# Tokens turned before their norm, three passes per half of a projection, and a list scheduler that is run again with latest times

## The chip, the cores and the metric

The kernel runs on one core of a Trainium2 chip. The metric is device time in microseconds of one execution; the time of a kernel is the median of several runs. The profile is of one further execution. Its engines are TensorE (PE; PEld is its weight load), VectorE (DVE), ScalarE (ACT), GpSimd (POOL) and SyncE (SP), which issues most transfers.

## The reference

One layer of a hybrid encoder is computed for two groups of tokens at once: 512 prompt tokens and 64 sample tokens, of width 1024, with shared weights.

```python
xn = _rmsnorm(x, p['ln_mix'])                 # x * rsqrt(mean(x*x) + EPS) * gain
proj = xn @ p['w_in']
conv_in, z, a, b, qd, kd, vd = jnp.split(proj, SPLIT_AT, axis=-1)
c, conv_new = _causal_conv(conv_in, p['conv_w'], conv_buf)
...
oa, S_new = _gdn_chunked(qa, ka, va, g, beta, S0)
...
ob = _diff_attention(qd, k_all, v_all, q_pos, k_pos, lam)
...
h = x + jnp.concatenate([oa, ob], axis=-1) @ p['w_out']
h = h + _mem_attn(_rmsnorm(h, p['ln_mem_q']), mem_k, mem_v, p['w_mem_q'], p['w_mem_o'])
hn = _rmsnorm(h, p['ln_ffn'])
h = h + jnp.square(jax.nn.relu(hn @ p['w_ff1'])) @ p['w_ff2']
```

The input projection has 3592 columns: twelve blocks of 128 for the convolution, four for the gate z, eight single columns for a and b, and twelve blocks for queries, keys and values of the attention. The norm of x is a factor per token, times a gain per feature.

## The kernel before

**Precision and layout.** Everything is in 32 bits. For a projection, weights w and inputs x are each split into a high and a low part (a cast to `fp32r` on ScalarE, a subtraction on VectorE), and high by high, high by low and low by high are summed in a PSUM bank. Inputs lie features by tokens: a 128-column weight block is the stationary operand, and the 576 tokens are streamed. `KT = 8` blocks k of 128 features are summed (`kt=4` in the second feed-forward product, which goes by groups of 512 features).

**A projection** (`project`, L463) goes by two halves of the tokens, `HALVES`: 0 to 255, and 256 to 575 (the last 64 are the sample). In the first half, `high_parts` (L479) streams the high and low inputs side by side, 2 by 256 columns, through one load of the high weight into a whole bank, and a second matmul of 256 columns adds low weight by high input. The eviction receives two sums, `b` and `more`, and adds them: `add_to` (L487) copies one on ScalarE and adds the other on VectorE. In the second half three matmuls of 320 columns go into one sum. The first feed-forward product (`ff1_pair`, L1767) is a scheme of its own with 288 columns per matmul; it is not edited.

**The opening** (L540 to L724) is written out by hand, `with in_order()`: each engine keeps the written order. Tokens are loaded five tiles at a time row by row (`load_x`), and the gain is spread over partitions by a matmul. Per tile: squares (ScalarE, L517), root (L522, and a power on GpSimd, L502), scaling with factor and gain (VectorE, L527), four turns on TensorE per half of the features (`turn`, L529, through `tr`, L411), and the split into high (`hi`, L582) and low (`lo`, L587). `first` multiplies three convolution blocks (4, 5 and 6) with the first 256 tokens as soon as these are there; `second` does their other 320 tokens. The convolution input leaves PSUM by copies on ScalarE (L612, L616, L617).

**The raw tokens** are needed once more, turned, as the residual. `raw_out` (L575) copies turned raw tokens out of PSUM (L577). Two groups of turns stand in the opening (L665, L685), eight more in the block behind the key convolutions (L765 to L768). The result goes to a scratch tensor `hd` and is read back as `hT` (L1505) before the output projection.

**After the input projection** come the chunked recurrence (`gdn_prep`, `gdn_scan`), with the gate z projected in between, and the attention, one head at a time: `diff_project` (L1261) projects q, k and v, and splits keys into two copies whose halves are moved across partitions by transfers (L1309, L1311). Then memory keys and values, the output projection and the memory attention (`add_residual`, `split_query`), and the feed-forward part: `ff1_pair` and `project` by groups (`add_group`, L1834), the last group by `last_block` (L1871). The end turns the result back, scales it and stores it.

**What sets the order.** The program is traced in one order. `arrange` (L304) builds an `Arrangement` of all instructions with a cost for each (`Step.cost`, L102), and runs a list scheduler once: at each step it takes the engine that can start first, and among what can start there the instruction of the smallest priority, then of the smallest number. The priority is that of the trace; `tc.high_priority()` stands around casts of weights (L454) and most evictions. Tiles come from pools with a fixed number of buffers per tag; projections have three banks (`pr`), the others two or one. The order found is laid down by dependences.

## Time and profile before

| what | value |
|---|---|
| median of 3 runs | 958.92 us (957.37 to 960.45) |
| the profiled execution | 958.01 us, span 956.1 us |
| mean granted TensorE clock | 0.997 |
| matmuls | 6399 |
| TensorE, VectorE, ScalarE busy | 945.9, 690.8, 536.4 us |
| bytes moved by transfers | 96.01 MB |

The span runs from the first to the last instruction of the program; the execution's time is longer by what lies around it. A row of the timeline gives start, time, engine, line, operation, output and inputs with shapes, how many were merged, and, in brackets, how long the engine stood idle before and what ended that. A matmul's time in such a row is that of one pass through the array, and consecutive ones overlap; what one costs in a stream is the distance from start to start. `pr`, `ba`, `g` and `gs` are PSUM banks.

### The profile page before, as it was taken

To read this page: it belongs to the slowest core of one execution; us is meant where nothing else is said; L and a number is where in the kernel's file an instruction comes from. 1 tells how busy PE (TensorE), PEld (TensorE's weight loads), DVE (VectorE), ACT (ScalarE), POOL (GpSimd) and SP (SyncE) were. 2 spreads that over 40 slices of the span, in tenths; PEclk is the share of its full clock that TensorE was granted. 3 is DMA by queue.
4 is the path that set the end of the run, shared out by engine and by line. 5 is a ranking of instruction groups with operands and counts; after the bars stand their busy time and mean duration, and the time that the engine had idled before them with its cause. 6 is when DMAs were issued, how large, how long until landed. Compare 5 with 4: busy or idle time off the path is not lost.

```text
span 956.1 us, 17017 instructions
## 1 busy us (share of the span) xinstructions
PE 945.9 (99%) x6399; PEld 889.0 (93%) x6399; DVE 690.8 (72%) x1538; ACT 536.4 (56%) x1246; POOL 68.2 (7%) x158
## 2 busy tenths in 40 slices
PE   9999999999999999999999999999999999999996
PEld 7999899999899888999999999999999999999996
DVE  5666786878678776656557978668867779978574
ACT  6665675444567765444445568666555544555444
POOL 4351020202010000000000000000000000000000
PEclk9999999999999999999999999999999999999998
DMA  6562322122656656331212423333323322222202
GB/s 193 135 212 67 81 66 67 45 68 69 155 136 167 221 170 198 86 113 45 66 45 61 129 88 89 101 88 90 88 68 89 89 87 88 89 90 89 66 23 99
DMA packets 124915, 96.01 MB, mean 100 GB/s; under 512 B 6204, under 2 KB 112846, under 8 KB 124322
## 3 DMA queue, kind: packets, MB, share of 16 engines
q1 hardware_dynamic: 124466, 94.28, 34.0%
q8 instruction: 50, 0.82, 0.4%
q10 hardware_dynamic: 368, 0.66, 0.2%
q14 instruction: 31, 0.25, 0.1%
HBM read 79.93 MB, written 9.75 MB: 94 GB/s over the span
## 4 chain that ended last, share of the span: by engine, by line
PE 92%; DMA 2%; issue 2%; DVE 2%; ACT 1%; POOL 0%; SPq 0%; POOLq 0%; ACTq 0%; DVEq 0%
PE pr L407 57%; PE ba L407 12%; PE g L407 12%; PE gs L407 7%; PE ba L411 2%; PE g L411 2%; DMA KQ<-vb 1%; DMA Dt<-At 1%; DMA u<-in_x_prompt_dram 0%; DMA out_dram<-p 0%; PE pr L411 0%; DVE wl L456 0%; DVE p L755 0%; ACT u L1897 0%; PE gs L411 0%
## 5 line engine op out<-in xcount | busy, mean ns | idle before, releaser
L407 PE MATMUL pr<-u,wh 128*128 128x320 f32 (+2 forms) x1240 | 326.3, 341 | 0.0
L407 PE MATMUL pr<-u,wl 128*128 128x256 f32 (+1 forms) x816 | 225.5, 301 | 0.0
L407 PEld LDWEIGHTS pr<-u,wh 128*128 128x128 f32 x1240 | 211.2, 188 | 14.4 <-ACT u L582 0.4
L407 PEld LDWEIGHTS pr<-u,wl 128*128 128x128 f32 x816 | 149.9, 189 | 2.6 <-DVE wl L683 0.2
L456 DVE TENSOR_TENSOR wl<-raw,wh 128x1024 fp32r<-128x1024 f32 x65 | 79.5, 1223 | 50.2 <-ACT wh L455 49.8
L455 ACT CAST wh<-raw 128x1024 fp32r<-128x1024 f32 x65 | 68.2, 1049 | 74.4 <-PE pr L407 63.9
L407 PE MATMUL pr<-u,w2h 128*128 128x320 f32 (+1 forms) x384 | 96.7, 339 | 0.0
L1755 ACT CAST w2h<-r 128x512 fp32r<-128x512 f32 x56 | 34.6, 620 | 71.4 <-PE pr L407 69.2
L407 PE MATMUL pr<-f,w2h 128*128 128x320 f32 (+1 forms) x288 | 72.3, 339 | 0.0
L407 PEld LDWEIGHTS pr<-u,w2h 128*128 128x128 f32 x384 | 65.1, 188 | 4.3
L407 PE MATMUL pr<-u,w2l 128*128 128x256 f32 (+1 forms) x256 | 65.2, 295 | 0.0
L407 PE MATMUL ba<-u,wl 128*128 128x288 f32 x360 | 52.7, 295 | 0.0
L407 PEld LDWEIGHTS pr<-f,w2h 128*128 128x128 f32 x288 | 48.8, 188 | 3.3
L502 POOL TENSOR_TENSOR tiny<-tiny,nhalf 128x1 f32<-128x1 f32 (+4 forms) x10 | 8.5, 849 | 605.5 <-DVE tiny L1911 506.8
L1845 DVE TENSOR_TENSOR u<-u,pr 128x256 f32<-128x256 f32 x96 | 42.8, 446 | 11.2 <-PE pr L407 10.8
L407 PEld LDWEIGHTS ba<-u,wl 128*128 128x128 f32 x360 | 49.4, 188 | 0.0
L407 PE MATMUL pr<-f,w2l 128*128 128x256 f32 (+1 forms) x192 | 48.8, 295 | 0.0
L407 PEld LDWEIGHTS pr<-u,w2l 128*128 128x128 f32 x256 | 47.0, 189 | 1.5
L1756 DVE TENSOR_TENSOR w2l<-r,w2h 128x512 fp32r<-128x512 f32 x56 | 38.4, 686 | 10.2 <-ACT w2h L1755 10.1
L407 PE MATMUL pr<-wh,u 128*128 128x512 f32 x128 | 42.0, 399 | 0.0
L1515 DVE TENSOR_TENSOR u<-u,pr 128x256 f32<-128x256 f32 (+1 forms) x48 | 21.6, 451 | 20.4 <-PE pr L407 20.4
L407 PEld LDWEIGHTS pr<-f,w2l 128*128 128x128 f32 x192 | 35.2, 189 | 1.1
(551 smaller groups left out, 2024.7 us busy)
## 6 DMA issues: line engine op xcount, KB each, us to landing
raw<-in_w_ff_dram SPq DMA_DIRECT2D x36, 512.0 KB
raw<-in_w_in_dram SPq DMA_DIRECT2D x28, 512.0 KB
r<-in_w_ff_dram SPq DMA_DIRECT2D x56, 256.0 KB
raw<-in_w_mem_k_dram SPq DMA_DIRECT2D x8, 512.0 KB
raw<-in_w_mem_v_dram SPq DMA_DIRECT2D x8, 512.0 KB
raw<-in_w_out_dram SPq DMA_DIRECT2D x8, 512.0 KB
raw<-in_w_mem_q_dram SPq DMA_DIRECT2D x8, 512.0 KB
raw<-in_w_mem_o_dram SPq DMA_DIRECT2D x8, 512.0 KB
```

The lines of the kernel that those rows point to most:

```text
L407: nc.tensor.matmul(out, lhsT, rhs, start=start, stop=stop, skip_group_check=skip_group_check)
L411: nc.tensor.transpose(out, in_, ident[:n, :n])
L455: A.copy(wh, raw)
L456: V.tensor_tensor(wl, raw, wh.bitcast(F32), ALU.subtract)
L502: G.tensor_tensor(out, in_, bc(nhalf[: in_.shape[0], 0:1], list(in_.shape)), ALU.pow)
L1515: V.tensor_tensor(hm, hm, b, ALU.add)
L1755: A.copy(wh, src)
L1756: V.tensor_tensor(wl, src, wh.bitcast(F32), ALU.subtract)
L1845: V.tensor_tensor(am, am, b, ALU.add)
```

## The change

The tokens are turned raw, once. High and low parts are made from the turned raw tokens times the gain; the norm's factor per token is computed beside it (`roots_of`), spread over the partitions by a matmul into a row `rB`, and multiplied at each eviction of the input projection (`scaled`). The same turned banks give the residual's copy (`raw_rows`). The projection's inputs are stored in another order of tokens: 0 to 255, the 64 sample tokens, 256 to 511 (`XCOL`), so that the input projection's halves are 320 and 256 columns (`GATHERED`); all other projections have two halves of 288 (`EVEN`). Each half takes three matmuls per k into one sum, and evictions handle one sum. Tokens and the first weights are loaded in halves by features. The opening isn't fixed by hand any more. The decay rows and the sample's state take other slots.

The scheduler gets other costs (transfers by their row length, half speed of TensorE in the first 9 us), prefers a more urgent instruction that is about to be ready over one that is ready, and is run nine times: after each run the latest time of every instruction that isn't TensorE's becomes its priority, and the run with the earliest end is taken.

```diff
+EVEN = ((0, T // 2), (T // 2, T // 2))
+XCOL = (0, 128, 320, 448, 256)
+GATHERED = ((0, 320), (320, 256))
...
+COLD = 9000.0
...
+    def choose(self, engines):
+        start, engine = min((self.start(s), e) for e in engines for s in self.queue[e])
+        urgency = lambda s: (s.priority, s.n)
+        s = min((s for s in self.queue[engine] if self.start(s) <= start), key=urgency)
+        if engine in ("ACT", "DVE", "POOL") and not s.is_dma and not s.boundary and s.time >= 200:
+            end, soon = start + s.time - OVERLAP[engine], []
+            for t in self.queue[engine]:
+                wait = self.start(t) - start
+                if 0 < wait <= 600 and end - self.start(t) > 0.5 * wait and urgency(t) < urgency(s):
+                    soon.append(t)
+            s = min(soon, key=urgency, default=s)
+        return s
...
+        for s in reversed(order):
+            delay[s.n] = max((delay[n] + time for n, time in behind.get(s.n, ()) if place[n] > place[s.n]), default=0.0)
+        return {n: self.last[0] - d for n, d in delay.items()}
+
+    def improve(self, rounds):
+        best = self.run(), self.order
+        for _ in range(rounds):
+            for n, at in self.latest().items():
+                if self.steps[n].engine != "PE":
+                    self.steps[n].priority = at
+            best = min(best, (self.run(), self.order), key=lambda b: b[0])
+        return best[1]
...
-    for instructions_of_engine in Arrangement(instructions, homes, closing, opening, chains).run().values():
+    for steps in Arrangement(instructions, homes, closing, opening, chains).improve(8).values():
...
-    def project(w, x, evac, kt=KT, halves=HALVES, between=None):
+    def project(w, x, evac, kt=KT, halves=EVEN):
...
+                xk = x[k // 4][:, :, k % 4, a0 : a0 + n]
+                mm(b[:, :n], w[1][:, k, :], xk[:, 0], start=k == 0, stop=False)
+                mm(b[:, :n], w[0][:, k, :], xk[:, 0], start=False, stop=False)
+                mm(b[:, :n], w[0][:, k, :], xk[:, 1], start=False, stop=k == kt - 1)
+            evac(b[:, :n], a0, n)
...
+    load_rows_of(0, 0)
+    load_first(4, 0, 4)
+    load_rows_of(0, 1)
+    load_first(4, 4, 8)
+    nc.sync.dma_start(xu[2][:DEC, 0, :], x_sample[0])
+    load_first(5, 0, 8)
+    load_first(6, 0, 8)
+    for q in range(2):
+        load_rows_of(1, q)
...
+    def scaled(dst, b, at):
+        V.tensor_tensor(dst, b, rB[: dst.shape[0], at : at + b.shape[-1]], ALU.mult)
...
+        for i in range(nk):
+            A.activation(his[i], b[:, i], AF.Identity, scale=gmix[:, k0 + i : k0 + i + 1])
+        for i in range(nk):
+            V.scalar_tensor_tensor(los[i], b[:, i], gmix[:, k0 + i : k0 + i + 1], his[i].bitcast(F32), ALU.mult, ALU.subtract)
+
+    def raw_rows(b, ts, k0, nk, n):
+        t0 = TT[ts[0]][0]
+        for q in range(k0 // 4, (k0 + nk - 1) // 4 + 1):
+            ks = slice(max(k0, 4 * q), min(k0 + nk, 4 * q + 4))
+            dst = hst[q][:, ks.start - 4 * q : ks.stop - 4 * q, t0 : t0 + n]
+            (V.tensor_copy if len(held) % 2 else A.copy)(dst, b[:, ks.start - k0 : ks.stop - k0])
+
+    def roots_of(ts):
+        for t in ts:
+            n = TT[t][1]
+            r1 = root(squares(junk[t % 2], xt[t], n), n)
+            b = bank("gs")
+            mm(b[:, :n], bc(r1[:n], [n, P]), ident[:n, :n])
+            V.tensor_copy(rB[:, XCOL[t] : XCOL[t] + n], b[:, :n])
+
+    keep_busy(3)
...
+    keep_busy(4)
...
+    for q, tags in enumerate((("ba", "ba"), ("g0", "g1"))):
+        banks = [turn_rows((0, 1), 4 * q + 2 * i, 2, tag) for i, tag in enumerate(tags)]
+        early += banks
+        for x in banks:
+            split_rows(*x)
+        cast_first(4, q)
+        first(4, (HH, Q[q]), (LH, Q[q]), (HL, Q[q]))
+    roots_of((0, 1))
+    early.append(turn_rows((4,), 0, KT, "gs"))
+    split_rows(*early[-1])
+    for q in range(2):
+        cast_first(5, q)
+    for x in early:
+        raw_rows(*x)
+    roots_of((4,))
+    ev[4](fb[4][:, :256], 0, 256)
+    first(5, (HH, K), (HL, K), (LH, K))
+    ev[5](fb[5][:, :320], 0, 320)
+    for q in range(2):
+        cast_first(6, q)
+    for k0, tag in enumerate(("ba", "ba", "g0", "g1")):
+        x = turn_rows((2, 3), 2 * k0, 2, tag)
+        split_rows(*x)
+        raw_rows(*x)
+    first(6, (HH, K), (HL, K), (LH, K))
+    ev[6](fb[6][:, :320], 0, 320)
+    roots_of((2, 3))
+    second(4)
...
-            with after(opened[mybir.EngineType.PE], opened[mybir.EngineType.Activation]):
-                for q in range(2):
-                    for t in range(0 if q else 2, 5):
-                        raw_out(t, q, turn(xt[t], TT[t][1], q, f"g{t % 2}"))
...
-        def evac(b, a0, n, more):
+        def evac(b, a0, n):
             am = (accu[0] if g < SCALED else hT)[m // 4][:, m % 4, a0 : a0 + n]
...
+                if g == 0:
+                    A.copy(am, b)
+                else:
+                    V.tensor_tensor(am, am, b, ALU.add)
```

`turn_rows` turns one or two token tiles for a range of features into one bank; `cast_first` splits half a weight tile; `first` now covers 256, 320 and 320 columns (`cut`), and `second` what is left.

More of the change, by code (lines that the diff above doesn't have):

```diff
@@ L204, in run @@
         for _ in range(len(todo)):
-            start, engine = min((self.start(s), e) for e in engines for s in self.queue[e])
-            s = min((s for s in self.queue[engine] if self.start(s) <= start), key=lambda s: (s.priority, s.n))
-            self.queue[engine].remove(s)
+            s = self.choose(engines)
+            self.queue[s.engine].remove(s)
             self.open_tiles(s)
-            end = self.execute(s)
-            if not s.boundary:
-                self.order[engine].append(s.inst)
+            self.began[s.n] = self.start(s)
+            end = self.ran[s.n] = self.execute(s)
+            self.order[s.engine].append(s)
             for t in s.after:
@@ L222, in run, with latest, edge @@
             self.close_tiles(s, end)
-        return self.order
+        return self.last[0]
+    def choose(self, engines):
[10 more added lines that the diff above has]
+        return s
+    def latest(self):
+        delay, behind = {}, {}
+        def edge(m, t, time):
+            behind.setdefault(m, []).append((t.n, time + (t.fetch if t.engine == "PE" else 0)))
+        order = sorted((s for steps in self.order.values() for s in steps), key=lambda s: self.began[s.n])
+        for s in order:
+            for m in s.before:
+                if m in self.began:
+                    p = self.steps[m]
+                    if p.engine != "PE" or s.engine != "PE":
+                        edge(m, s, self.ran[m] - self.began[m] + (0 if p.engine == s.engine else 33))
+        for m, s in self.handed:
+            edge(m, s, self.ran[m] - self.began[m] + 33)
+        for s, t in zip(self.order["PE"], self.order["PE"][1:]):
+            behind.setdefault(s.n, []).append((t.n, s.step * s.passes))
+        place = {s.n: i for i, s in enumerate(order)}
+        for s in reversed(order):
[9 more added lines that the diff above has]
+        return best[1]
     def tag_in_the_way(self, s):
@@ L266, in close_tiles @@
                 tag["free"].append(self.ended[t])
+                self.freed[self.place[t][0], self.ended[t]] = s.n
                 self.readmit(tag)
@@ L304, in arrange @@
 def arrange(tc, instructions, homes, chains, closing, opening):
-    for instructions_of_engine in Arrangement(instructions, homes, closing, opening, chains).run().values():
-        for earlier, later in zip(instructions_of_engine, instructions_of_engine[1:]):
+    for steps in Arrangement(instructions, homes, closing, opening, chains).improve(8).values():
+        steps = [s.inst for s in steps if not s.boundary]
+        for earlier, later in zip(steps, steps[1:]):
             tc.add_manual_dep(
@@ L629, in keep_busy, with cast_first, first @@
             mm(idle[:, :P], ones, ones)
+    def cast_first(m, q):
+        ks = slice(4 * q, 4 * q + 4)
+        hi, lo = (list(w)[q] if m == 6 else w[:, ks] for w in wts[m])
+        A.copy(hi, raws[m][:, ks])
+        V.tensor_tensor(lo, raws[m][:, ks], hi.bitcast(F32), ALU.subtract)
     fb = {}
-    def first(m, *order):
+    def first(m, *steps):
         if m not in fb:
             fb[m] = bank("pr")
-        for pw, px in order:
-            for k in range(KT):
-                mm(
-                    fb[m][:, :256], wts[m][pw][:, k, :], xs[k // 4][:, px, k % 4, :256],
-                    start=(pw, px) == HH and k == 0, stop=(pw, px) == LH and k == KT - 1,
+        n = cut[m]
+        for (pw, px), ks in steps:
+            for k in ks:
+                mm(
+                    fb[m][:, :n], wts[m][pw][:, k, :], xs[k // 4][:, px, k % 4, :n],
+                    start=(pw, px) == HH and k == 0, stop=(pw, px) == steps[-1][0] and k == KT - 1,
                 )
     def second(m):
-        a0, n = HALVES[1]
+        a0, n = cut[m], T - cut[m]
         b = bank("pr")
@@ L726, in hybrid_layer_kernel, with turn_rows @@
-    with after(opened[mybir.EngineType.Pool]):
+        ev[m](b[:, :n], a0, n)
+    held = []
+    def turn_rows(ts, k0, nk, tag):
+        b = bank(tag)
+        n = sum(TT[t][1] for t in ts)
+        for i in range(nk):
+            for j, t in enumerate(ts):
+                m = TT[t][1]
+                tr(b[:, i * n + j * P : i * n + j * P + m], xt[t][:m, (k0 + i) * P : (k0 + i + 1) * P])
+        held.append((b[:, : nk * n].rearrange("p (k n) -> p k n", k=nk), ts, k0, nk, n))
+        return held[-1]
@@ new lines, in hybrid_layer_kernel @@
+    keep_busy(3)
+    b = bank("gs")
+    tr(b[:, :KT], gain)
+    gmix = const([P, KT], "gmix")
+    V.tensor_copy(gmix, b[:, :KT])
+    keep_busy(4)
+    x4 = small("zr", [P, 320]), small("zr", [P, 320])
+    K, Q = range(KT), (range(4), range(4, 8))
+    ev = {m: conv_input(m, "an" if m == 6 else "cb") for m in FIRST}
+    early = []
+    for q, tags in enumerate((("ba", "ba"), ("g0", "g1"))):
[5 more added lines that the diff above has]
+        first(4, (HH, Q[q]), (LH, Q[q]), (HL, Q[q]))
@@ L727, in hybrid_layer_kernel @@
+    first(6, (HH, K), (HL, K), (LH, K))
+    ev[6](fb[6][:, :320], 0, 320)
+    roots_of((2, 3))
+    second(4)
+    gps = bank("g0")
+    tr(gps[:, :126], rows)
+    gcol = const([P, 126], "gcol")
+    V.tensor_copy(gcol, gps[:, :126])
+    with after(last_traced()):
         G.memset(triu, 1.0)
```

318 lines of the change are left out of this document (110 added, 208 removed).

## The prediction

> **What bounds the kernel now.** I read the page first, then busy time by stage, then the chain of waits, then the timeline of TensorE in the places that the change touches.
>
> ```profile
> span 956.1 us, 17017 instructions
> PE 945.9 (99%) x6399; PEld 889.0 (93%) x6399; DVE 690.8 (72%) x1538; ACT 536.4 (56%) x1246; POOL 68.2 (7%) x158
> PE 92%; DMA 2%; issue 2%; DVE 2%; ACT 1%; POOL 0%; SPq 0%; POOLq 0%; ACTq 0%; DVEq 0%
> ```
>
> TensorE is busy 99% of the span and holds 92% of the chain that ended last. So three things can change the time: what TensorE issues, how slowly it starts, and the few places where its stream is broken. The busy share hides the start, since a slow matmul counts as busy too.
>
> ```profile
> core 0: us, PE busy (x) PEld busy (x) DVE busy (x) ACT busy (x) POOL busy (x), PEclk, DMA share, GB/s
> 0.00:28.10 28.10, 26.80 (x157) 22.20 (x158) 16.53 (x23) 17.56 (x33) 10.40 (x22) 1.00 0.75 207
> 105.00:240.00 135.00, 134.75 (x1039) 127.17 (x1037) 104.65 (x277) 74.42 (x171) 19.80 (x40) 1.00 0.25 65
> 240.00:345.00 105.00, 103.99 (x673) 93.63 (x672) 77.87 (x238) 69.18 (x225) 7.19 (x15) 1.00 0.58 168
> 513.00:904.00 391.00, 391.00 (x2693) 378.85 (x2692) 300.64 (x602) 219.55 (x485) 0.00 (x0) 1.00 0.30 90
> 904.00:957.00 53.00, 44.47 (x299) 42.01 (x297) 31.32 (x68) 25.73 (x50) 1.55 (x2) 0.94 0.16 55
> ```
>
> The count tells what the share does not: 157 matmuls in the first 28 us, 1039 in the 135 us of the third row. The end (8.5 us without TensorE, of 53) is computed after the last projection and is not edited.
>
> **Part 1: three passes per half.** A projection now issues five matmuls per block k of the contraction: in the first half a merged one of 512 columns and one of 256, in the second three of 320. After the change it is six: three of 288 twice (output, memory query, memory output, feed-forward) or three of 320 and three of 256 (input projection). Columns per k stay 1728. So only what a matmul costs beyond its columns can differ.
>
> ```profile
> 592.26 12.69 PE pr L407 x80
> 604.95 1.59 PE ba L407 x12
> ```
>
> The first row is four feed-forward projections of four k each, 16 k in 12.69 us, 0.793 us per k. The second is twelve 288-column matmuls of the layer before it, 0.1325 us each; six make 0.795. That is 2 ns more per k. There are 24 projections of 8 k and 56 of 4 k in this form, 416 k: +0.8 us, with 0 to 2 as bounds, for the rounding of 1.59.
>
> ```profile
> 16.07 1.12 PE L407 MATMUL pr<-u,wh 128*128 128x256 f32 x8
> 17.02 0.65 PE L411 MATMUL g<-ident,u 128*128 128x128 f32 x4
> 24.55 1.34 PE L407 MATMUL pr<-u,wh 128*128 128x320 f32 x8
> 25.73 1.33 PE L407 MATMUL pr<-u,wl 128*128 128x320 f32 x8
> 28.07 0.27 PE L411 MATMUL g<-ident,B 126*128 126x126 f32 x1
> ```
>
> From start to start, eight matmuls of 256 columns take 0.95 us (0.119 each) and eight of 320 take 1.18 (0.147; 24 of them fill the 3.52 us up to the last row). Three of each make 0.798 against 0.793: 5 ns more. Nine convolution, four gate and twelve attention projections of 8 k are 200 k: +1.0 us. The last block's first half (32 k) and the small a/b projection (8 k) add under 0.2. Part 1 costs **+1.8 us**, between 0.5 and 3.
>
> The Trainium skill, "TensorE: Matmul & The Clock Gate", section "Back-to-back issue gap", speaks against this edit: a warm matmul costs its columns over 2.4 GHz plus 2.5 ns, so each of the 656 matmuls added (416, 200, 32 and 8) costs 2.5 ns; by it the part would cost an estimated 1.6 us. That agrees with 2 to 5 ns per k from the rows.
>
> Evictions become lighter outside the input projection: no copy of a second sum and no second add. While TensorE runs back to back (391 us busy of 391) that is worth nothing. In the input projection ScalarE copies become VectorE products with the factor row.
>
> ```profile
> 24.23 0.40 DVE L587 TENSOR_TENSOR u<-gs,u 128x256 fp32r<-128x256 f32 x1
> ```
>
> The nearest row, a two-operand step of 256 columns out of PSUM, takes 0.40 us; there are two per projection of 6.4 us (8 k). VectorE was busy 104.65 of 135 us there; an added 0.4 to 0.8 us per projection leaves it below TensorE, so I take nothing for it and keep +1 us as a bound.
>
> **Part 2: the raw tokens are turned once.** Today normalised tokens are turned for the projection and raw ones again for the residual, eight groups of four in the middle of a saturated stream.
>
> ```profile
> L411 PE MATMUL g<-ident,u 128*128 128x128 f32 x24 | 3.4, 272 | 0.0
> L411 PE MATMUL g<-ident,u 64*128 64x64 f32 x8 | 0.9, 234 | 0.0
> 41.56 1.03 PE L411 MATMUL g<-ident,u 128*128 128x128 f32 x8
> 42.35 0.49 PE L407 MATMUL pr<-u,wh 128*128 128x512 f32 x1
> 43.95 0.46 PE L411 MATMUL g<-ident,u 64*128 64x64 f32 x4
> 44.34 0.51 PE L407 MATMUL pr<-u,wh 128*128 128x512 f32 x1
> ```
>
> Eight turns hold the stream for 0.79 us, 0.1 each; four of 64 tokens, with a short wait, 0.39. 24 by 0.1 and two groups by 0.39 make **-3.2 us**, between 2.8 and 4.3 (the busy time of both groups). The raw copies out of PSUM move into the opening (part 3 counts them). The two stores to the scratch tensor stay behind the key convolutions in the program; on SP they can only go earlier, ahead of weight loads that have 6.4 us per projection, so they cost nothing. Tiles that merely change their slot (decay rows, state) cost nothing either.
>
> **Part 3: the opening.** Today the turns wait for the norm: tokens, squares, root, scaling, turn.
>
> ```profile
> 5.25 1.06 ACT L517 ACTIVATE u<-u 128x1024 f32<-128x1024 f32 x1 [0.18 <-DMA u<-in_x_prompt_dram]
> 6.58 1.06 ACT L517 ACTIVATE u<-u 128x1024 f32<-128x1024 f32 x1 [0.18 <-DMA u<-in_x_prompt_dram]
> 8.58 1.05 ACT L669 CAST wh<-raw 128x1024 fp32r<-128x1024 f32 x1 [0.85 <-DMA raw<-in_w_in_dram]
> 7.36 0.75 DVE L527 SCALAR_TENSOR_TENSOR u<-u,tiny,gmix 128x512 f32<-128x512 f32 x1 [0.48 <-POOL tiny L502]
> 6.08 2.08 PE L407 MATMUL g<-ident,u 128*128 128x128 f32 x8
> 8.17 1.12 PE L411 MATMUL pr<-ident,u 128*128 128x128 f32 x4
> 11.07 0.95 PE L411 MATMUL ba<-ident,u 128*128 128x128 f32 x4
> 11.95 2.67 PE L407 MATMUL pr<-u,wh 128*128 128x256 f32 x16
> ```
>
> The first tokens are there at 5.2, the next 0.5 MB 1.3 us later, the first weights at 8.5; the first projection starts at 11.95 and its 24th matmul ends near 17.0 (the row quoted above). The new load order sends the same bytes in halves: half the depth of 256 tokens by 5.2, half the weights 1.0 later, the rest at 7.5 and 8.5, then the sample tokens (0.65), two weight tiles (2.0 each) to 13.2, the last tokens at 15.8.
>
> Without the norm ahead, turns start at 5.2. Eight at the slow 0.21 us (the row at 6.08) end at 6.9, eight more from 7.5 end between 8.4 and 9.2. Then come the splits.
>
> ```profile
> 23.69 0.36 ACT L582 CAST u<-gs 128x256 fp32r<-128x256 f32 x1
> 10.63 0.68 DVE L587 TENSOR_TENSOR u<-pr,u 128x512 fp32r<-128x512 f32 x1
> 28.38 0.29 DVE L724 COPY gcol<-g 128x126 f32<-128x126 f32 x1 [2.22 <-PE g L411]
> 8.03 0.15 DVE L522 TENSOR_SCALAR tiny<-tiny 128x1 f32<-128x1 f32 x1
> ```
>
> After 0.36 us on ScalarE, four VectorE splits of 256 columns (0.40, as above) and half a weight cast (0.68) are 2.3 us from about 8.8: the first projection is complete near 11.5, not 17. Behind it on TensorE, up to the end of that projection's second half (today 28.10): two projections of 24 by 0.147 (7.1), sixteen turns by 0.11 and eight small ones by 0.08 (2.4), the second half (3.5), and new matmuls that spread the norm factor over partitions, five of two passes by 0.11 (1.1). That is 14.1, so 25.6 if it never waits: 2.5 sooner. And more is done by then: those two projections now take 320 columns first, which leaves their second halves 48 times 147 less 119 ns shorter, 1.3 us. Together **-3.8 us**.
>
> Bounds: if TensorE never waits from 5.2, the first sixteen turns (1.8, and 0.8 more for eight slow ones), the first 24 products (2.9) and the 14.1 end at 24.8: -4.6. VectorE bounds the other side: sixteen splits and four of the sample (20 by 0.4), six weight halves and six raw copies by 0.68, two raw copies and five evictions by 0.4, five roots with a copy of the factor by 0.15 + 0.29: 21.2 us. From 6.3, behind the first ScalarE split, that ends at 27.5, 0.6 sooner: -1.9. So the opening is nearly bound by VectorE, where today it was busy 16.53 of 28.1.
>
> What was turned once no longer takes the factor before the split, so each eviction waits for the factor row: squares, a power on GpSimd, a matmul and a copy. Queued behind an eviction are later splits on VectorE; TensorE waits only when its three projection buffers are full, by the fourth product, near 20 us. Squares can run from 5.2 on, 1.06 us each: the cover is long.
>
> **Part 4: the scheduler.** The order of all engines but TensorE is now drawn from latest times, nine runs, the best by its own model. What it can win are the breaks in the stream.
>
> ```profile
> PE g L407 <- DMA Dt<-At: 1.0, 1, 1.0
> PE ba L407 <- DVE gg L845: 0.2, 1, 0.2
> 246.16 0.38 SPq L451 DMA_DIRECT2D raw<-in_w_in_dram  x1
> 247.36 5.97 DMA Dt<-At
> ```
>
> One wait is worth 1.0 us: the doubled key rows of the first attention head, 5.97 us in the transfer queue, where a weight load issued at 246.16 goes first. The wait view knows one more, 0.2. By the stage table the third and fourth stages lose 0.25 and 1.01 us outright. An order by latest times should send the key rows first: **-1.0 us**, between -3 (waits that hide in stretched matmul steps) and +2 (new ones).
>
> **The sum.** +1.8 - 3.2 - 3.8 - 1.0 = -6.2 us. The profiled execution took 958.01 us, 1.9 of it around its span; it becomes 951.8. The median of the runs, 958.92, is 0.9 above it, so I expect **952.7 us**, 0.65% faster. A measurement here can tell 0.3%, 2.9 us, from no change.
>
> **The rivals.**
>
> *The opening gives little and the scheduler nothing.* Two ways lead there. VectorE takes the norm's place: 21.2 us of work before 27.5, and one late microsecond in the input projection. That is +1.8 - 3.2 - 1.9 + 1 + 0 = -2.3, 956.6 us, no change. Against it: today's VectorE idles 11.6 of the first 28.1 us, and raw copies can wait. Or the half clock stays: 0.21 per turn at 6.08, still 0.22 at 11.07 (four turns up to 11.95), 0.119 for 256 columns at 16.07. If it lasts as long as today, the first 24 products run slow and cost 24 by 0.12, 2.9 us: +1.8 - 3.2 - 0.9 + 0 = -2.3, again 956.6 us. The Trainium skill, "TensorE: Matmul & The Clock Gate", section "What's actually happening", says that the full clock comes after some 3.4 us of sustained work and goes again in idle time; by that rule the warming matmuls at the start decide, and the trace agrees that the slow part ends only once turns follow closely. Against it: part of the slow time falls into the wait for VectorE before 11.5. Both together 0.18.
>
> *The casts lose their urgency.* Today weight casts carry a hard priority; by latest time they run just before TensorE wants them, on a model that can be wrong.
>
> ```profile
> L1756 DVE TENSOR_TENSOR w2l<-r,w2h 128x512 fp32r<-128x512 f32 x56 | 38.4, 686 | 10.2 <-ACT w2h L1755 10.1
> ```
>
> The place is the feed-forward stage, 56 tiles. If each came late by a third of its 0.69 us, TensorE would wait 13 us: 958.92 - 6.2 + 13 = 965.7 us, slower. It decides from 9.1 us of such waits on. Against it: VectorE is busy 300.64 of 391 us there and the change lightens it, so work that is ready seldom queues. 0.07.
>
> *The breaks go altogether.* Opening -4.6, scheduler -3, passes +0.8, turns -3.6: -10.4, 948.5 us. For it: the stage table's stretched stages. Against: only two waits are named. 0.13.
>
> That the change does not do what it says can be so only for the scheduler, if its first run stays the best: then -5.2, within my forecast, which has 0.62.
>
> **How the numbers follow.** My forecast's own bounds, with not all unknowns at one end at once, are -2 and -9: 950 to 957 us. The no-change rival lies at its upper edge, the large gain below. The range of 8 in 10 is 947.5 to 958: it leaves out the slower case and the ends of the others. Faster takes the 0.13 and the 0.62, 0.75, since the small part of the forecast above 956 and that of the rival below it cancel; same 0.18; slower 0.07.
>
> **What would show it.** Right: no raw turns near 42 us; the second half of the first projection ending near 25.6 us; 16 k of a feed-forward projection in 12.72 us instead of 12.69; no wait of 1 us for the key rows. Wrong: feed-forward groups split by waits for the casts; a k of the input projection above 0.81 us; a turn at 0.21 us after 10 us; VectorE without a gap from 6 to 27 us with TensorE waiting for it.

## The result, and the profile after

The changed kernel takes 970.36 us (median of 5 runs, 968.71 to 971.75), the kernel before 958.73 us beside it (957.37 to 960.45): 1.0122 times as long, with an interval of 1.0105 to 1.0139. The forecast was 952.7 us. The profiled execution took 970.35 us, its span is 968.3 us.

First the page of the changed kernel: span, busy times, shares of the chain that ended last.

```profile
span 968.3 us, 18136 instructions
PE 948.3 (98%) x7028; PEld 924.8 (96%) x7028; DVE 681.8 (70%) x1528; ACT 519.6 (54%) x1176; POOL 63.2 (7%) x154
PE 70%; issue 2%; DVE 1%; DMA 1%; ACT 0%; SPq 0%; POOLq 0%; POOL 0%; DVEq 0%; ACTq 0%
```

TensorE's busy time rose by 2.4 us only, but the span by 12.2. So most of the loss is time in which TensorE does not work. The busy time by stage, for the stages shown of before, says where.

```profile
0.00:28.10 28.10, 22.57 (x127) 20.64 (x128) 15.11 (x39) 16.69 (x37) 3.76 (x16) 0.82 0.75 213
105.00:240.00 135.00, 134.43 (x1116) 131.44 (x1114) 111.65 (x298) 69.46 (x158) 19.20 (x40) 1.00 0.24 63
240.00:345.00 105.00, 98.28 (x669) 91.24 (x668) 71.74 (x236) 59.38 (x194) 6.13 (x13) 0.97 0.51 147
513.00:904.00 391.00, 391.00 (x2949) 390.12 (x2948) 290.11 (x566) 225.15 (x495) 0.00 (x0) 1.00 0.31 91
```

The opening has 127 matmuls in 28.1 us where before had 157, and a granted clock of 0.82 where it was 1.00. The attention heads (240 to 345 us) have TensorE idle for 6.7 us where it was 1.0, and a clock of 0.97. The feed-forward stage is as full as it was. The wait view of TensorE names the same two places:

```profile
PE g L474 <- DMA u<-in_x_prompt_dram: 3.8, 1, 3.8
PE g L470 <- DMA out_dram<-vs: 2.5, 1, 2.5
PE g L470 <- ACT p L1411: 2.4, 1, 2.4
PE g L470 <- issue: 1.3, 1, 1.3
```

To place the loss I summed the columns of the large matmuls (256, 288, 320 and 512 columns) in order of their start, and read when the sum passes a mark. This table is worked out from the matmul records of the traces; the experiments in it follow below. Before streams 2,048 columns more (the gain spread by four matmuls of 512 in the opening), which is 0.9 us at 0.1325 us per 288; so +0.9 in the table is level. e7 still streams them, and for it 0 is level. Each column is one execution: e7 issues TensorE's work in the order of before up to 369 us, and still reads up to 1.7 us less there, so a difference under 2 us in one column says little.

| thousand columns | before, us | after | e4 | e6 | e13 | e7 |
|---|---|---|---|---|---|---|
| 50 (opening done) | 38.19 | +4.57 | +4.33 | +0.69 | +1.52 | -0.67 |
| 100 (raw turns of before done) | 64.76 | +1.19 | +0.95 | -2.69 | -1.86 | -0.67 |
| 190 | 109.29 | +2.29 | +2.05 | -1.59 | -0.76 | -0.67 |
| 450 (heads done) | 335.18 | +13.14 | +2.19 | +10.20 | -0.58 | -1.66 |
| 500 | 362.37 | +12.16 | +2.88 | +9.13 | +0.35 | -1.66 |
| 1700 | 927.70 | +13.53 | +4.28 | +10.54 | +1.81 | -1.15 |

After is 3.7 us late at the end of the opening, wins 3.4 where before turns its raw tokens, and loses 10.9 between 190 and 450 thousand columns, in the recurrence and the heads.

Now the two places on TensorE's timeline. The heads first, with the transfers that SyncE's queue issued just before:

```profile
242.86 1.25 SPq L1366 DMA_DIRECT2D Dt<-At  x2
249.67 0.46 SPq L1368 DMA_DIRECT2D At<-At  x1
```

TensorE's own rows there, and the third such wait 74 us later:

```profile
246.92 0.31 PE L470 MATMUL pr<-u,wl 128*128 128x320 f32 x1
249.74 0.41 PE L470 MATMUL g<-Dt,qs 128*128 128x128 f32 x2 [2.51 <-DMA out_dram<-vs]
251.98 0.66 PE L470 MATMUL g<-At,qs 128*128 128x128 f32 x2 [1.34 <-issue]
323.34 0.30 PE L470 MATMUL g<-kd,qs 128*128 128x128 f32 x1 [2.36 <-ACT p L1411]
```

All three late products read doubled key rows (`Dt`, `At`, `kd`), which a transfer moves across partitions. The releaser that the profile names (a store, an old ScalarE step, "issue") is not what they read. The signals by which the key rows' transfers report their landing are in the trace too: the last of them comes at 249.60, 251.89 and 323.25 us, 0.09 to 0.14 us before the product that reads the rows. So the operands end the waits. TensorE is at the first 4.4 us behind the issue of its rows and gets them 6.9 us behind it. It is at the second 1.0 us behind the issue and starts 2.3 behind it; that transfer overwrites what the first one reads, and was issued 0.07 us behind its landing. The three waits make 6.2 us. Behind the first two the clock goes down, by the stage view of after (the third last number is PEclk):

```profile
252.00:260.00 8.00, 8.00 (x45) 8.00 (x46) 2.31 (x12) 2.12 (x9) 0.00 (x0) 0.64 0.21 63
319.00:330.00 11.00, 8.61 (x57) 7.07 (x56) 4.41 (x13) 4.87 (x14) 1.35 (x3) 1.00 0.99 352
```

At 0.64, eight busy microseconds did the work of 5.1, so 2.9 us more are lost there without any idle time. 6.2 and 2.9 are 9.1 of the 10.9. Behind the third wait, in the second row, the clock stays at 1.00.

The opening of after, on the same timeline, and the stage view of its slow part:

```profile
4.99 0.37 PE L474 MATMUL ba<-ident,u 128*128 128x128 f32 x1 [0.59 <-DMA u<-in_x_prompt_dram]
5.45 0.98 PE L474 MATMUL ba<-ident,u 128*128 128x128 f32 x7
10.19 1.97 PE L474 MATMUL g<-ident,u 128*128 128x128 f32 x8 [3.76 <-DMA u<-in_x_prompt_dram]
17.08 1.05 PE L470 MATMUL pr<-u,wl 128*128 128x256 f32 x4
17.93 1.03 PE L470 MATMUL pr<-u,wh 128*128 128x256 f32 x4
18.89 0.71 PE L474 MATMUL gs<-ident,u 64*128 64x64 f32 x8
```

```profile
8.00:10.20 2.20, 0.01 (x1) 0.02 (x1) 0.20 (x1) 0.34 (x1) 0.00 (x0) 0.63 1.15 256
10.20:18.60 8.40, 8.26 (x36) 7.59 (x36) 6.51 (x16) 7.97 (x17) 1.12 (x2) 0.50 0.68 214
```

The first eight turns start 0.2 us sooner than forecast. Then TensorE waits 3.76 us for the other half of the features, the clock falls to half during that wait, and stays there for at least 8.4 us of work: at 17.08 four matmuls of 256 columns take 0.85 us from start to start, 0.21 each, where 0.119 is the full rate. The first projection ends at 18.9 us.

### The profile page after: what moved, and what is told of

Its sections match the earlier page's. It is cut to its first block, busy times and chain, and to the rows that moved or that the text cites. A ratio compares the mean times of both kernels' runs of the same rounds, so it can differ in the third digit from the quotient of the medians.

```text
span 968.3 us, 18136 instructions
## 1 busy us (share of the span) xinstructions
PE 948.3 (98%) x7028; PEld 924.8 (96%) x7028; DVE 681.8 (70%) x1528; ACT 519.6 (54%) x1176; POOL 63.2 (7%) x154
## 4 chain that ended last, share of the span: by engine, by line
PE 70%; issue 2%; DVE 1%; DMA 1%; ACT 0%; SPq 0%; POOLq 0%; POOL 0%; DVEq 0%; ACTq 0%
PE pr L470 44%; PE ba L470 11%; PE g L470 8%; PE gs L470 5%; PE ba L474 2%; DMA out_dram<-vs 1%; DMA p<-in_cache_diff_k_dram 0%; DVE ta L1450 0%; ACT p L1453 0%; DVE u L1944 0%; POOLq L2061 0%; DVE p L1458 0%; SPq L1366 0%; DVE g L1449 0%; POOL tiny L544 0%
## 5 line engine op out<-in xcount | busy, mean ns | idle before, releaser
L470 PE MATMUL pr<-u,wh 128*128 128x288 f32 (+2 forms) x1632 | 354.8, 308 | 0.1
L470 PEld LDWEIGHTS pr<-u,wh 128*128 128x128 f32 x1632 | 269.3, 191 | 2.0 <-ACT wh L662 0.5
L470 PE MATMUL pr<-u,wl 128*128 128x288 f32 (+2 forms) x816 | 247.3, 309 | 0.0
L470 PE MATMUL pr<-u,w2h 128*128 128x288 f32 x512 | 102.1, 295 | 0.0
L470 PEld LDWEIGHTS pr<-u,w2h 128*128 128x128 f32 x512 | 81.8, 188 | 0.0
L470 PE MATMUL pr<-f,w2h 128*128 128x288 f32 x384 | 76.5, 295 | 0.0
L470 PE MATMUL pr<-u,w2l 128*128 128x288 f32 x256 | 75.5, 295 | 0.0
L470 PE MATMUL pr<-f,w2l 128*128 128x288 f32 x192 | 56.5, 294 | 0.0
L1892 DVE TENSOR_TENSOR u<-u,pr 128x288 f32<-128x288 f32 x96 | 43.2, 450 | 15.3 <-PE pr L470 15.1
L1807 DVE TENSOR_TENSOR w2l<-r,w2h 128x512 fp32r<-128x512 f32 x56 | 38.5, 689 | 12.6 <-ACT w2h L1806 12.2
L1572 DVE TENSOR_TENSOR u<-u,pr 128x288 f32<-128x288 f32 (+2 forms) x48 | 21.7, 453 | 20.9 <-PE pr L470 19.4
```

The source lines that it names most:

```text
L470: nc.tensor.matmul(out, lhsT, rhs, start=start, stop=stop, skip_group_check=skip_group_check)
L1572: V.tensor_tensor(hm, hm, b, ALU.add)
L1807: V.tensor_tensor(wl, src, wh.bitcast(F32), ALU.subtract)
L1892: V.tensor_tensor(am, am, b, ALU.add)
```

## The experiments

Each number is a median, with the ratio to runs of before on the same chip and its 95% interval. Differences between two experiments are those of the medians; against the changed kernel, which ran on its own beside before, the ratios give up to 0.6 us less or more (6.8 for the 7.4 us of the scheduler below, 8.9 for the 9.5 of the transfer cost, 11.2 for the 10.6 of the repetition). Two theories stood against each other first. *Scheduler*: the heads lose by the new scheduler. *Program*: they lose by the edits (products by the factor row at evictions, halves of 320 and 256).

**e1 and e2: each alone.** e1 is the new program under the old scheduler (the class `Arrangement` and `Step.cost` of before), e2 the old program under the new one.

```diff
-    for steps in Arrangement(instructions, homes, closing, opening, chains).improve(8).values():
+    for instructions_of_engine in Arrangement(instructions, homes, closing, opening, chains).run().values():
```

> The program of after (raw tokens turned once, three passes, factor at evictions, new load order) under the old scheduler: one run, trace order as urgency, old costs. Scheduler theory (the 11 us lost between 240 and 345 us belong to the new scheduler): 957 to 960 us, the last product of the first attention projections for the sample within 2 us of before's 335 us. Program theory (the edits to the evictions and the order of the 256 and 320 columns lose it): 968 to 971 us.

> The program of before under the new scheduler (nine runs, latest times as urgency, new costs). Scheduler theory: 968 to 971 us, with waits of TensorE for doubled key rows of 1 to 3 us between 240 and 345 us. Program theory: 957 to 960 us.

e1: 962.95 us, 1.0051 (1.0036 to 1.0066). e2: 973.76 us, 1.0170 (1.0147 to 1.0192), above its range. The scheduler loses the heads on either program (e2 loses 6.6 us from 190 to 450 thousand columns, e1 1.5); e2's wait view of TensorE has the same kind of line:

```profile
PE g L467 <- DMA At<-At: 5.0, 1, 5.0
```

But e1 is above its range too: the program alone loses 4.8 us, where parts 1 to 3 of the forecast gain 5.2. Its opening is 3.4 us late by the columns, nearly as late as that of after, so the new scheduler is not what makes the opening slow.

**e3 and e4: which part of the scheduler.** e3 leaves out the repetition, e4 puts the old cost of a transfer back.

```diff
-    for steps in Arrangement(instructions, homes, closing, opening, chains).improve(8).values():
+    for steps in Arrangement(instructions, homes, closing, opening, chains).improve(0).values():
```

```diff
-            alone, queued = s.rates
-            self.wire = max(at + 1300 + s.bytes / alone, self.wire + s.bytes / queued)
-            return self.wire
+            begin = max(at + 1300, self.wire)
+            self.wire = begin + s.bytes / 240.0
+            return max(self.wire + 500, at + 1900)
```

> After with the scheduler's first run alone: new costs, but trace order as urgency throughout. If the repetition with latest times loses the time: 957 to 960 us. If the new, more hopeful cost of transfers loses it: 968 to 971 us, with the same waits for key rows as after.

> After with nine runs and latest times, but each transfer costed as in before (240 bytes per ns one after the other, never under 1.9 us, 0.5 us until it is seen). If the cost of transfers loses the time: 957 to 960 us and no wait above 1 us for doubled key rows. If the repetition loses it: 968 to 971 us.

e3: 980.95 us, 1.0245 (1.0227 to 1.0263), above both cases: repetition wins 10.6 us, it does not lose. e4: 960.84 us, 1.0027 (1.0016 to 1.0038), just above its range: the cost of transfers loses 9.5 us. By the table e4 is like after up to 190 thousand columns and loses 0.1 us from there to 450, where after loses 10.9. The same first product of `Dt` on e4's timeline, its transfers first, then TensorE:

```profile
241.90 1.19 SPq L1366 DMA_DIRECT2D Dt<-At  x2
```

```profile
247.96 0.28 PE L470 MATMUL pr<-u,wl 128*128 128x256 f32 x1
249.03 0.86 PE L470 MATMUL ba<-both,p 128*128 128x128 f32 x6
249.65 0.42 PE L470 MATMUL g<-Dt,qs 128*128 128x128 f32 x2
249.91 0.33 PE L470 MATMUL pr<-u,wl 128*128 128x256 f32 x1
```

It starts at 249.65 us, as in after at 249.74, but without a wait: the stream of the second half's products stands ahead of it. The rows were issued 1 us earlier only, and the first transfer took about as long (6.1 us to its last signal, 6.4 in after). What differs is the place that TensorE's fixed order gives the product. The plans that the two schedulers make for it (they follow from the code of the kernels, and no trace holds them) show why: for this transfer, queued behind others, after's plan has 4.7 us from issue to landing and e4's has 8.3. One is too short and the other too long, and only the short one makes TensorE wait.

**e5, e6, e16: what in that cost.** e5 keeps the new rates and puts the floor back; e6 keeps all new costs but leaves SyncE's priorities as traced; e16 is more careful than the old cost.

```diff
# e5
-            return self.wire
+            return max(self.wire + 500, at + 1900)
# e6
-                if self.steps[n].engine != "PE":
+                if self.steps[n].engine not in ("PE", "SP"):
# e16, against e4
-            self.wire = begin + s.bytes / 240.0
-            return max(self.wire + 500, at + 1900)
+            self.wire = begin + s.bytes / 200.0
+            return max(self.wire + 1500, at + 2900)
```

> After with nine runs and the new byte rates of transfers, but with the old floor put back (0.5 us until a transfer is seen, never under 1.9 us after its issue). If the missing floor lets TensorE's order put the products of doubled key rows too early: 960 to 963 us, no wait above 1 us for key rows. If the faster rates (320 bytes per ns in a queue where the old cost had 240) do it: 967 to 971 us, with such waits.

> After, new costs, but the transfer queue keeps the trace order as urgency while ScalarE, VectorE and GpSimd take latest times. Theory (TensorE's fixed order is drawn on transfers that land too early in the model): 967 to 972 us still. Rival (latest times put weight loads and stores ahead of the key rows in the queue): 958 to 962 us.

> After with nine runs and a transfer cost more careful than the old: 200 bytes per ns, 1.5 us until it is seen, never under 2.9 us. New cost 970, new with old floor 966, old 961 us so far. If hopeful transfers are still what the heads lose by: 957 to 960 us. If the old cost is careful enough: 959.5 to 962.5 us.

e5: 965.66 us, 1.0078 (1.0064 to 1.0092), between the two cases, with one wait of 3.2 us for key rows left: floor and rates lose about half each. e6: 966.49 us, 1.0081 (1.0067 to 1.0095), just under its range: the rival of a badly ordered queue falls, since e6 loses 11.8 us from 190 to 450 thousand columns. (It gains 3.9 in the opening; below.) e16: 965.10 us, 1.0076 (1.0063 to 1.0090), a miss. It loses nothing more in the heads (+3.09 at 190, +2.10 at 450 thousand), but 1 us in the opening and 5.1 from 450 to 520 thousand, where e4 loses 0.8. TensorE idles 2.0 us of that stretch, 1.2 of them in one wait for the low part of a weight. So a more careful cost loses 4.3 us against e4, elsewhere than the hopeful one.

**e10, e11, e15: the other costs.** e10 is e2 with the old transfer cost, e11 is e4 with one run, e15 is e11 without the look-ahead.

```diff
-        if engine in ("ACT", "DVE", "POOL") and not s.is_dma and not s.boundary and s.time >= 200:
+        if False and not s.is_dma and not s.boundary and s.time >= 200:
```

> The kernel of e2 (before's program, new scheduler) with transfers costed as in before. If the transfer costs are what loses, 12 to 17 us come back: 956 to 961 us. If latest times lose by themselves on this program: over 965 us.

> After with old transfer costs and the first run alone (no latest times). With e4 it gives what repetition is worth when the costs of transfers are careful. If repetition wins 10 us as it does on the new costs (e3 against after): 970 us. If it only mends what the hopeful costs spoil: 961 to 964 us.

> The kernel of e11 (one run, old transfer costs) without the look-ahead by which an engine stays free for a more urgent step that will be ready within 0.6 us. If the look-ahead, on trace order as urgency, is what loses 11 us against the old scheduler (e1): 961 to 965 us. If the other new costs do it: 971 to 976 us.

e10: 965.97 us, 1.0088 (1.0074 to 1.0102): 7.8 us come back on the old program too, but 8 stay lost, which is its second case (over 965 us). 6.4 us of them are lost by 100 thousand columns already; which part of the new scheduler loses them on the old program was not tested. e11: 973.97 us, 1.0167 (1.0153 to 1.0181), above both cases. So repetition wins 13.1 us with old transfer costs, yet one run of the new scheduler is 11.0 worse than the old scheduler's one run (e1). e15: 970.30 us, 1.0130 (1.0117 to 1.0144): the look-ahead makes 3.7 of these 11, a result between its two cases; the rest lies in what else the two schedulers do differently (costs of TensorE's steps, half speed before 9 us, SyncE's start), and was not taken apart further. Against the old scheduler, nine runs with the old transfer cost win 2.1 us (e1 to e4).

Over all runs the heads divide by the transfer cost. From 190 to 450 thousand columns the five kernels planned with the new rates there (after, e2, e3, e5, e6) lose 6.6 to 17.4 us, and all others lie between -1.3 and +3.4, whatever the program, the repetition or the look-ahead.

**e7: the passes.** Before, with a projection of its own for the output, memory and second feed-forward projections:

```diff
+            for k in range(kt):
+                xk = x[k // 4][:, :, k % 4, a0 : a0 + n]
+                mm(b[:, :n], w[1][:, k, :], xk[:, 0], start=k == 0, stop=False)
+                mm(b[:, :n], w[0][:, k, :], xk[:, 0], start=False, stop=False)
+                mm(b[:, :n], w[0][:, k, :], xk[:, 1], start=False, stop=k == kt - 1)
+            evac(b[:, :n], a0, n, None)
```

> Before, old scheduler, with three passes of 288 columns twice in the output, memory and second feed-forward projections (416 k) in place of merged ones; the input projection is left merged. Prediction's part 1: 0.8 us slower, 0 to 2 as bounds: 958.5 to 960.5 us, a k of six matmuls in 0.795 us. Rival (lighter evictions give time back): 956 to 958 us.

958.89 us, 1.0006 (0.9997 to 1.0015): +0.6 us where 0.8 was forecast, but the interval, -0.3 to 1.4, holds zero. From 500 to 1,700 thousand columns it loses 0.5. A group of 16 k on its chain of waits (start, duration, engine, bank, matmuls):

```profile
590.67 12.72 PE pr L407 x96
```

**e8, e9, e13, e14: the opening.** Here the theories were: TensorE's half clock sets its pace; the landing of the tokens does; or the order does. e8 is e4 with eleven more idle products at the start, costed at nothing, so that the order stays; e9 joins e4 and e6; e13 is e9 with the new transfer cost before 30 us; e14 is e13 with five more idle products.

```diff
# e8 (e14: 9 in place of 15)
-    keep_busy(4)
+    keep_busy(15)
# e13
+            if at < 30000:
+                alone, queued = s.rates
+                self.wire = max(at + 1300 + s.bytes / alone, self.wire + s.bytes / queued)
+                return self.wire
```

> The kernel of e4 (after, old transfer cost) with the same order on every engine, and eleven more of the idle products of ones at the start, so that TensorE does not stand still until the first tokens are there. If the throttle's half clock between 8 and 21 us, which follows TensorE's waits, is what ate the gain of the opening: granted clock 1.00 from 7 to 14 us, 956 to 958.5 us, 2 to 4 us under e4. Rival (the transfers set the pace of the opening whatever the clock): within 1 us of e4, 959.5 to 961.5 us.

> After with both changes that helped one stage each: transfers costed as in before (e4) and the transfer queue in trace order (e6). If the two losses (the opening of after, the attention heads) are separate, this opens like e6 (50 thousand columns of products near 39 us instead of 42.8) and runs the heads like e4: 956 to 958.5 us. If the opening of e6 came from its own order by chance: 959 to 961 us.

> The kernel of e9, but with the new transfer costs for what is planned before 30 us and the old ones behind: this plans the opening of e6 and the heads of e9. If the opening's order decides (first pair of tokens turned before the first products): 50 thousand columns near 39 us as in e6, 3 us before e9, and 956 to 958 us in all. If e6 opened well by chance of its transfers: within 1 us of e9, 959.5 to 961.5 us.

> The kernel of e13 with the same order and five more of the idle products of ones at the start, so that TensorE works until the first tokens are there. If half clock from 5 to 11 us is what makes the first projection end near 14.5 us: turns and products at full clock from the start, 1.5 to 3 us under e13. If ScalarE's and VectorE's splits set that pace: within 0.7 us of e13.

e8: 959.55 us, 1.0019 (1.0010 to 1.0028), 1.3 under e4, at the edge of the rival's range: the clock stays at 1.00 to 17 us, and 1.1 us of the opening come back by the table's count (+3.19 at 50 thousand). e9: 960.40 us, 1.0023 (1.0014 to 1.0032): heads as in e4, opening not as in e6 (+4.07 at 50 thousand). e13: 958.25 us, 1.0004 (0.9995 to 1.0013): e6's opening order, planned again, gives most of its early start again (+1.52), so it is the order; the time is just above the expected range. e9 issues the same transfers in the same order there, but puts eleven products before the second eight turns. On its timeline e13 turns all sixteen blocks of the first 256 tokens before it multiplies much:

```profile
5.63 1.97 PE L478 MATMUL ba<-ident,u 128*128 128x128 f32 x8 [0.88 <-DMA u<-in_x_prompt_dram]
7.69 0.58 PE L474 MATMUL pr<-u,wh 128*128 128x256 f32 x1
8.07 1.91 PE L478 MATMUL g<-ident,u 128*128 128x128 f32 x8
13.65 1.02 PE L474 MATMUL pr<-u,wh 128*128 128x256 f32 x4
14.60 0.71 PE L478 MATMUL gs<-ident,u 64*128 64x64 f32 x8
```

Its first projection ends at 14.6 us. e14: 957.57 us, 0.9997 (0.9988 to 1.0006), level with e13. Its timeline:

```profile
6.36 1.09 PE L482 MATMUL ba<-ident,u 128*128 128x128 f32 x8
9.36 1.09 PE L482 MATMUL g<-ident,u 128*128 128x128 f32 x8 [1.20 <-DMA u<-in_x_prompt_dram]
15.04 1.02 PE L478 MATMUL pr<-u,wh 128*128 128x256 f32 x4
```

Turns at full clock (0.11 each), but the other half of the tokens comes later than in e13, from the same queue, and the first projection ends at 16.0. This traced execution took 959.80 us, the slowest of e14's eleven, so it can't say what the median's opening looks like. The medians of e13 and e14 are 0.7 us apart and their intervals overlap, so full clock at the start alone is not worth the 1.5 to 3 us expected of it: half clock is not the one bound.

**e12, e17, e18: ScalarE's part.** On e13's timeline ScalarE has no gap from 6.5 to 14.9 us. These are rows of that stretch:

```profile
7.17 0.95 ACT L725 ACTIVATE u<-ba,gmix 128x256 fp32r<-128x256 f32 x2
8.01 1.05 ACT L563 ACTIVATE u<-u 128x1024 f32<-128x1024 f32 x1
9.05 0.83 ACT L725 ACTIVATE u<-ba,gmix 128x256 fp32r<-128x256 f32 x2
9.77 1.06 ACT L563 ACTIVATE u<-u 128x1024 f32<-128x1024 f32 x1
11.16 0.63 ACT L666 CAST wh<-raw 128x512 fp32r<-128x512 f32 x1
11.67 1.23 ACT L725 ACTIVATE u<-g,gmix 128x256 fp32r<-128x256 f32 x3
```

e12 (on e9) and e17 (on e13, same order) take the squares over 64 of 1024 columns and so leave out most of the norm's sum, to see what their time is worth; e18 moves half of the scaled copies of the first 256 tokens to VectorE.

```diff
# e12, e17
-            r1 = root(squares(junk[t % 2], xt[t], n), n)
+            r1 = root(squares(junk[t % 2][:, 960:], xt[t][:, 960:], n), n)
# e18
+            if i % 2 and ts[0] == 0:
+                V.tensor_scalar(his[i], b[:, i], gmix[:, k0 + i : k0 + i + 1], None, ALU.mult)
+            else:
```

> The kernel of e9 with the sums of squares of the input norm taken over 64 of the 1024 columns (part of the computation is left out): ScalarE has five steps of about 0.2 us in place of about 1.1. If ScalarE's queue (two squares, eight scaled copies, two casts ahead of the last split) sets the end of the first projection, near 14.6 us in e6: that end comes 1.5 to 2.5 us sooner and the run is 1 to 2.5 us under e9. If the landing of the tokens or TensorE's half clock sets it: within 0.7 us of e9.

> The kernel of e13, same order on every engine, with the sums of squares of the input norm over 64 of 1024 columns (part of the computation is left out). If ScalarE's queue sets the end of the first projection: it ends 1.2 to 2 us sooner than e13's 14.6 us, 50 thousand columns near 38 us, 956 to 957.3 us in all. If the landing of the tokens or half clock sets it: within 0.5 us of e13, 957.8 to 958.8 us.

> The kernel of e13 with four of the eight scaled copies of the first 256 tokens on VectorE in place of ScalarE (same result; the order is planned anew). If the splits set the pace and the shared work helps: the first projection ends near 13 us and the run takes 955.5 to 957.5 us, under before. If VectorE's own queue takes the place of ScalarE's: within 0.7 us of e13; over 959 us if the new order opens worse.

e12: 959.88 us, 1.0019 (1.0010 to 1.0028). e17: 958.02 us, 1.0002 (0.9993 to 1.0011). e18: 959.01 us, 1.0012 (1.0003 to 1.0021). None gets faster by more than can be told: ScalarE's queue alone does not set the pace. The first projection ends at 15.7, 15.5 and 14.7 us. In each trace something else is late next. In e18 TensorE waits 0.4 us for VectorE's copies. In e17 TensorE has half clock up to 13 us (10.5 in e13), and on VectorE the last four splits stand behind a copy that waits for a matmul of the factor row:

```profile
12.68 0.29 DVE L744 COPY rB<-gs 128x128 f32<-128x128 f32 x1 [2.12 <-PE gs L475]
```

So each run takes one limit away while another stands. Full clock from the start and a shorter ScalarE queue together were not run.

## Why the prediction was wrong, step by step

Parts 3 and 4 failed by about 8 us each; by the forecast's sum of -6.2, either alone would have turned a gain into a loss.

**Part 4 failed.** The step was "An order by latest times should send the key rows first: -1.0 us", with +2 as its bad end. The scheduler costs 7.4 us on the new program (e1 to after), and its hopeful transfer cost, which shows in the heads, loses more than all of that: 9.5 (after to e4). The mechanism is not where I looked: I read the new order of the queue and not the new cost. The diff took out the floor and raised the rate from 240 to as much as 394 bytes per ns; a lone transfer of 128 KB of key rows, 2 KB per row, is planned to land 1.3 us and 131,072 bytes by 272 per ns behind its issue, 1.8 us in all, where the old cost gave 2.3. In a queue the rate counts for more: 4.7 us in after's plan against 8.3 in e4's for the rows of the first wait, which took 6.4 and 6.1. The row that I quoted, 5.97 us for such a transfer, was the number to hold against the new cost. A list scheduler that believes the short time puts the reader too early, and TensorE's fixed order waits. That waits can also bring half clock behind them was not in my price for a wait at all. And the wait of 1.0 us that I hoped to win is not in e7's trace, which has the same order of TensorE there: it was no property of the order.

**Part 3 failed.** The step was "the first projection is complete near 11.5, not 17". It ends at 18.9 us in after, where a turn at 0.21 us after 10 us, one of my signs of being wrong, stands in the trace (10.19), and between 14.6 and 16.0 in the five other openings whose end is given here. The opening, forecast at -3.8 us, came at +3.7. Two mistakes are in it. I let the other half of the tokens land at 7.5 us; TensorE had it at 10.2 in after, at 8.1 or before in e13 and at 9.4 in e14. And I counted one ScalarE step of 0.36 us ahead of the splits, where eight scaled copies, two squares and two casts stand, and VectorE's 11.6 idle us, on which I relied, were a sum over the stretch and not a gap at the right time. What holds the end near 15 us stays open: with full clock (e14), with 1.6 us less on ScalarE (e17) or with its copies shared (e18) the end came no sooner, at 16.0, 15.5 and 14.7. The rival "half clock stays" came near, but by another way: it let the slow start last, and in after the clock was full for the first turns and fell again in the wait for tokens. Its price was 2.9 us; e8, which keeps the clock full, is 1.3 us faster than e4.

**Part 1 held** as far as it was tested. 12.72 us per 16 k, as forecast, on the chain of waits of after:

```profile
604.31 12.72 PE pr L470 x96
```

e7 gives 0.6 us, not clear of zero, for the 416 k forecast at 0.8. The 200 k of the input projection were not tested alone; in after's trace one of them takes 0.80 us (0.36 for 256 columns, 0.44 for 320), where 0.798 was forecast. That the Trainium skill's 2.5 ns per matmul, which I quoted, gave nearly the same sum was luck: its formula makes a matmul of 288 columns 122.5 ns, where the rows have 132.5. **Part 2 held**: 3.4 us between 50 and 100 thousand columns, 3.2 forecast. The evictions' extra products cost nothing that shows: TensorE is busy 134.43 of 135 us in the third stage's row.

The slower rival had the wrong place. Casts did not lose their urgency: TensorE is busy 391.00 of 391 us in the feed-forward stage. Its own condition, a model that can be wrong, was the right suspicion; I applied it to casts, and not to transfers, whose costs the change edits.

With both losses reduced (e13, e14) the kernel is level with before, not 0.65% faster. In e13 the opening is 0.6 us late, the raw turns give 3.4, and the rest of the new program takes 3.7 again from 100 to 1,700 thousand columns: the passes, 1.8 by the forecast, and about 2 that I did not place and that one execution can hardly tell. No version here beats before by more than can be told.

## What to carry to other kernels

If a change edits the cost model of a scheduler, hold each new cost against the traced duration of that thing in the stage where it binds. A consumer in a fixed order must not be placed before its transfer lands there under load; a longer cost is safe for that consumer, but not free elsewhere (970, 961 and 965 us for the hopeful, the old and a still more careful cost). No run here planned with the traced durations themselves. Price a wait of TensorE at its length plus the half clock that can follow it. For an opening, lay each engine's steps in a row, since idle time summed over a stretch is not idle time where it is needed.

## What the runs showed of the hardware that was not expected

Half clock behind a wait can last long. In after the clock falls at 8.56 us, 2.1 us into a wait of 3.76, and TensorE then works for at least 8.4 us at 0.50. In the heads, waits of 2.5 and 1.3 us, 0.9 apart, were enough for a mean of 0.64 over the 8 us from 252 us on; the wait of 2.36 us at 321 us was followed by full clock. By the traces' records of the clock, every stretch of half clock ahead of the last one of its run lasted 3.41, 6.83 or 10.24 us (10.24 and 6.83 in after). Half of that is lost if TensorE works through it, an estimate of 1.7 to 5.1 us. The Trainium skill, "TensorE: Matmul & The Clock Gate", section "What's actually happening", gives about 3.4 us, one window, for either step, the idle and the busy one. The steps of 3.41 us fit it. But the clock fell after 2.1 us of idle time, and stayed low for 8.4 us of work, where one window of either would have been 3.4; there the measurement decides.

The profile's clock does not show the slow start: e13's first stage reads 1.00, while eight turns from 5.63 us take 1.97, as long as the eight at half clock in after.

```profile
0.00:28.10 28.10, 25.88 (x154) 23.45 (x155) 18.44 (x50) 17.57 (x38) 4.11 (x18) 1.00 0.71 210
```

Only the distance from start to start tells.

The same transfer of half the tokens' features lands at quite different times. In after it was issued third behind the first and TensorE had it at 10.19 us; in e13, in nearly the same queue, at 8.07 or before; and in e14, whose queue had issued the same transfers in the same order as e13's, at 9.36. So the order of the queue does not explain it, and what does was not tested.
